# High and low weight halves in one buffer, with placements of their own for stationary and moving use

## The chip, the cores and the metric

The kernel runs on one core of a Trainium2 chip. The metric is device time in microseconds (us), the median of several executions of the whole program, from the first instruction to the last.

## The reference

Two decoder layers over 256 tokens of width 2048, batch 1, all in float32. Layer 0 mixes tokens with sparse attention (compressed blocks, selected blocks and a sliding window, gated), layer 1 with a chunkwise mLSTM. After each mixer comes a gated convolution FFN of width 5632, and a normalisation ends it.

```python
for i in range(DEPTH):                       # DEPTH = 2
    xn = rms_norm(x, norm_mix[i])
    y = nsa_mixer(...) if i % 2 == 0 else mlstm_mixer(...)
    x = x + y
    x = x + conv_glu_ffn(rms_norm(x, norm_ffn[i]), ffn_w_up[i], ...)
return rms_norm(x, norm_final)
```

In `nsa_mixer` the attention scores, of queries with compressed and with plain keys, are multiplied by `hd ** -0.5`, here `QSCALE`. Nearly all of the arithmetic is products of the 256 x K activations with large weight matrices.

## The kernel before

**Products in three parts.** TensorE's fast float32 type (`fp32r`) is not exact enough alone, so every big operand is kept as a high half (the value rounded to `fp32r`) and a low half (the rest). A product is the sum of three matmuls: high x high, low x high and high x low. The activations stand transposed in `xh` and `xl` (16 k-tiles of 128 partitions x 256 tokens). Mixer outputs stand in `oh`, `ol` (called `moh`, `mol` in the mLSTM), the FFN's hidden values in `gh`, `gl`, laid out in the same way.

**Weights on the way in.** `load_split` loads a piece of 128 partitions x up to 1024 columns from HBM into `raw` (4 buffers, DMA issued by SyncE). ScalarE writes the high half into `whi` (line 192) and VectorE the low half into `wlo` (line 194), with 5 buffers each. The pieces are split ahead of TensorE in program order; a buffer is handed on when its last reader is done.

**Three users of a piece.**

- `cols_piece` (lines 228, 230, 231) has the weights stationary and the activations moving, 256 columns: per k-tile and 128 output columns it multiplies `whi` with `xh`, `whi` with `xl` and `wlo` with `xh`. Query and key projections and the FFN's up projection take it, 24 matmuls to a piece.
- `rows_times` has the weights moving and `xh`, `xl` stationary, by `rows_mm` (lines 200 to 202): `xh` with `whi`, `xh` with `wlo`, `xl` with `whi`. It makes the value and gate projections, with 256, 304, 412, 416 or 512 columns a matmul.
- `project_out` uses `rows_mm` too, with `oh`, `gh` or `moh` (and their low halves) stationary: output projections and the FFN's down projection, 512 columns a matmul (256 in the last one for the second half of the tokens), 12 matmuls to a piece.

While a matmul streams its moving operand, the stationary operand of the next one is loaded.

**Where things lie.** A pool's tiles stand one behind the other in each partition, and buffers of a tile in a row; small unused `pad_` tiles shift what follows. `xh` and `xl` take 16384 bytes each, a multiple of 256. Counted from them, in bytes modulo 256:

| tile | before | after |
|---|---|---|
| `xh`, `xl` | 0 | 0 |
| `raw` | 64 | 0 |
| high half, weights stationary | 64 | 64 |
| low half, weights stationary | 192 | 192 |
| high half, weights moving | 64 | 0 |
| low half, weights moving | 192 | 0 |
| `oh`, `gh`, `moh` | 64 | 0 |
| `ol`, `gl`, `mol` | 192 | 0 |
| step from one weight buffer to the next, bytes | 4096 | 8448 = 33 x 256 |

In the attention's gather (lines 601 to 603) the probabilities `ph`, `pl` move, 512 columns, over the stationary values `vh`, `vl`; all four stand at one phase, before and after.

**Order of work.** Each engine runs its own instructions in program order. Side work (attention units, mLSTM heads, evacuations of accumulators) is put between pieces by a queue (`tick`). The lines that the steps below speak of: `load_split` 181 to 196, `rows_mm` 198 to 202, `rows_times` 205, `cols_piece` 221 to 232, `project_out` 312, `k_out` 424, `rq` 445, `compressed` 495, `q_out` 507.

Of the kernel before, what the change touches and what calls it, by code (L numbers as in the profile page):

```python
# [21 lines left out]
P = 128  # L22
# [40 lines left out]
def trunk(ctx: ExitStack, tc: tile.TileContext, x, positions, nsa_w_in, nsa_gate_b, nsa_cmp_pe,  # L63
# [10 lines left out]
    wpool = ctx.enter_context(tc.tile_pool(name="wpool", bufs=1))  # L74
    wpool.tile([P, 16], F32, name="pad_w")
    small = ctx.enter_context(tc.tile_pool(name="small", bufs=2))
# [4 lines left out]
    def nm(s):  # L81
        uid[0] += 1
        return f"{s}_{uid[0]}"
# [91 lines left out]
    def preload(w, k0, nk, c0, n):  # L175
        ready[w.tensor.name, w.offset, k0, c0] = load_split(w, k0, nk, c0, n)

    apart = []

    def load_split(w, k0, nk, c0, n):  # L180
        got = ready.pop((w.tensor.name, w.offset, k0, c0), None)
        if got is not None:
            return got
        view = lambda t: t[:, :nk * n].rearrange("p (k c) -> p k c", k=nk)
        raw = wpool.tile([P, 1024], F32, name=nm("raw"), tag="raw", bufs=RAWB)
        nc.sync.dma_start(view(raw), w[k0 * P:(k0 + nk) * P, c0:c0 + n].rearrange("(k p) c -> p k c", p=P))
        hi = wpool.tile([P, 1024], F32R, name=nm("whi"), tag="whi", bufs=SPB)
        if not apart:
            apart.append(wpool.tile([P, 32], F32, name="pad_lo"))
        lo = wpool.tile([P, 1024], F32R, name=nm("wlo"), tag="wlo", bufs=SPB)  # L190
        with queued("act"):
            latest["act"] = act(view(hi), view(raw), AF.Copy).ins  # L192
        with queued("ve"):
            latest["ve"] = ve.tensor_sub(view(lo), view(raw), fview(view(hi))).ins  # L194
        return view(hi), view(lo)
# [24 lines left out]
    def cols_piece(ps, w, c0, k0, n):  # L220
        hi, lo = load_split(w, k0, n, c0, 256)
        run_hooks()
        for i in range(n):
            for j in range(2):
                kt = k0 + i
                a = hi[:, i, j * P:(j + 1) * P]
                b = lo[:, i, j * P:(j + 1) * P]
                mm(ps[:, j, :], a, xh[:, kt, :], start=(kt == 0 and j == 0), stop=False,  # L228
                   skip_group_check=True)
                mm(ps[:, j, :], a, xl[:, kt, :], start=False, stop=False, skip_group_check=True)  # L230
                mm(ps[:, j, :], b, xh[:, kt, :], start=False, stop=(kt == KT - 1 and j == 1),  # L231
                   skip_group_check=True)
        tick()
# [115 lines left out]
    def nsa(norm, nxt):  # L349
        with tc.tile_pool(name="nsa", bufs=1) as pool, tc.tile_pool(name="nsw", bufs=2) as wk:  # L350
# [13 lines left out]
            gate = pool.tile([P, NT, 48], F32, name="gate")  # L364
            rq = pool.tile([P, S], F32, name="rq")
            hid = pool.tile([P, 2, 32], F32, name="hid")
# [4 lines left out]
            nc.gpsimd.memset(fview(pct), 0.0)  # L371
            pool.tile([P, 32], F32, name="pad_oh")
            oh = pool.tile([P, HEADS, S], F32R, name="oh")
            pool.tile([P, 32], F32, name="pad_ol")
            ol = pool.tile([P, HEADS, S], F32R, name="ol")
# [48 lines left out]
            def k_out(b, ps):  # L424
                ve.tensor_mul(kr[:, :, b, :], ps, norm.rbc2)
                rope(kr[:32, :, b, :], kr[:32, :, b, :])
# [11 lines left out]
            def vw_out(accs):  # L438
# [5 lines left out]
                act(gate, gate, AF.Sigmoid)  # L444
                ve.tensor_scalar(rq, norm.rbc, QSCALE, None, op0=ALU.mult)

# [48 lines left out]
            def compressed():  # L495
                ps = bank()
                mm(ps[:, :32], w2[:, 0, :], hid[:, 0, :], start=True, stop=True)
                ve.tensor_copy(kcmp.rearrange("p g j -> p (g j)"), ps[:, :32])
                ps = bank()
# [7 lines left out]
            def q_out(pair, ps):  # L507
                qu = wk.tile([P, 2, S], F32, name=nm("qu"), tag="qu", bufs=3)
                qr = wk.tile([P, 2, S], F32, name=nm("qr"), tag="qr", bufs=3)
                ve.tensor_mul(qu, ps, rq[:, None, :].to_broadcast([P, 2, S]))  # L510
                act(qr, qu, AF.Copy)
                rope(qr[:32], qu[:32])
                q[pair] = (qu, qr)
# [167 lines left out]
    def mlstm(norm, nxt):  # L681
        with tc.tile_pool(name="mls", bufs=1) as pool, tc.tile_pool(name="mlw", bufs=2) as wk:
# [6 lines left out]
            nc.gpsimd.memset(v1[:, :, :, DV:DV + 1], 1.0)  # L689
            pool.tile([P, 48], F32, name="pad_m")  # L690
            oh = pool.tile([P, KT, S], F32R, name="moh")
            pool.tile([P, 32], F32, name="pad_n")
            ol = pool.tile([P, KT, S], F32R, name="mol")
# [166 lines left out]
    def ffn(layer, norm, nxt):  # L860
        with tc.tile_pool(name=f"ffn{layer}", bufs=1) as pool, tc.tile_pool(name=f"ffw{layer}", bufs=2) as wk:
            pool.tile([P, 16], F32, name=f"pad_f{layer}")
            pads = []
            wu, wd = ffn_w_up[layer], ffn_w_down[layer]
# [18 lines left out]
            def up(ffs):  # L883
                gh = wk.tile([P, 8, S], F32R, name=nm("gh"), tag="gh")
                if not pads:
                    pads.append(wk.tile([P, 32], F32, name=f"pad_g{layer}", tag="pad_g", bufs=1))
                gl = wk.tile([P, 8, S], F32R, name=nm("gl"), tag="gl")
# [118 lines left out]
```

## Time and profile before

| what | us |
|---|---|
| median of 3 runs | 2188.14 (2188.11 to 2188.83) |
| the profiled execution | 2189.75 |
| its span, first to last instruction | 2188.0 |
| TensorE matmuls busy | 2170.5 (99%) |
| VectorE busy | 1441.2 (66%) |
| ScalarE busy | 1114.1 (51%) |
| mean granted TensorE clock, as a share of full speed | 0.996 |

A matmul's shown duration includes the way through the array and overlaps the next one, so durations of matmuls don't add up to time; the distance between starts does. What the profile calls idle before an instruction is time in which its engine ran nothing, with the event that ended it. A timeline row gives the start, the shown length, the engine, the line and the tiles.

### The profile page before, as it was taken

What the parts mean: (1) busy time and instruction counts of PE and PEld (TensorE: products, weight loads), DVE (VectorE), ACT (ScalarE), POOL (GpSimd) and SP (SyncE); (2) the same over time, 40 slices, a digit from 0 to 9 for tenths busy, and PEclk for the clock granted to TensorE, in tenths of its full rate; (3) what the DMA queues carried; (4) which work ended last, traced back from release to release, by engine and by line L of the source; (5) the groups of instructions that cost most, each with busy time, mean ns of one, the idle gap of its engine ahead of it and who ended that gap; (6) DMA issues with size and microseconds to landing.
All of it is one profiled execution on the core that took longest, in us unless ns stands there. A gap on an engine that the chain in (4) does not pass through costs nothing.

```text
span 2188.0 us, 37284 instructions
## 1 busy us (share of the span) xinstructions
PE 2170.5 (99%) x15072; PEld 1999.7 (91%) x15072; DVE 1441.2 (66%) x2191; ACT 1114.1 (51%) x1565; POOL 19.2 (1%) x56
## 2 busy tenths in 40 slices
PE   9999999999999999999999999999999999999998
PEld 8898789999989899998899988889999898998986
DVE  7488757776657666675645666667676576675755
ACT  6366655554545454453654444555545454454543
POOL 2000000000000000000000000000000000000000
PEclk9999999999999999999999999999999999999999
DMA  7653345666666666666566555566666666666664
GB/s 243 203 174 107 106 162 181 197 193 193 193 192 193 191 195 192 193 194 189 161 189 202 173 173 172 171 200 194 194 193 193 191 195 190 193 193 191 192 192 133
DMA packets 298317, 403.33 MB, mean 184 GB/s; under 512 B 12904, under 2 KB 256840, under 8 KB 298016
## 3 DMA queue, kind: packets, MB, share of 16 engines
q1 hardware_dynamic: 297264, 399.03, 58.8%
q8 instruction: 118, 1.93, 0.4%
q0 software_dynamic: 688, 1.83, 0.3%
q14 instruction: 55, 0.45, 0.1%
q10 hardware_dynamic: 192, 0.08, 0.0%
HBM read 398.80 MB, written 2.10 MB: 183 GB/s over the span
## 4 chain that ended last, share of the span: by engine, by line
PE 97%; ACT 1%; DVE 1%; DMA 1%; issue 0%; SPq 0%; ACTq 0%
PE bank L228 18%; PE bank L231 18%; PE bank L230 18%; PE bank L201 13%; PE bank L200 13%; PE bank L202 13%; PE bank L553 1%; PE bank L262 1%; ACT pr L557 0%; ACT whi L192 0%; PE bank L584 0%; DVE wlo L194 0%; DMA h<-in_x_dram 0%; PE bank L528 0%; DMA raw<-in_nsa_w_in_dram 0%; PE bank L602 0%
## 5 line engine op out<-in xcount | busy, mean ns | idle before, releaser
L194 DVE TENSOR_TENSOR wlo<-raw,whi 128x1024 fp32r<-128x1024 f32 (+3 forms) x755 | 911.8, 1209 | 591.7 <-ACT whi L192 590.6
L192 ACT ACTIVATE whi<-raw 128x1024 fp32r<-128x1024 f32 (+3 forms) x755 | 791.2, 1049 | 913.7 <-PE bank L230 429.1
L228 PE MATMUL bank<-xh,whi 128*128 128x256 f32 x3456 | 959.3, 278 | 3.1 <-ACT whi L192 1.9
L231 PE MATMUL bank<-xh,wlo 128*128 128x256 f32 x3456 | 956.1, 277 | 1.5 <-DVE wlo L194 1.5
L230 PE MATMUL bank<-xl,whi 128*128 128x256 f32 x3456 | 956.3, 277 | 0.2 <-DVE xl L268 0.2
L228 PEld LDWEIGHTS bank<-xh,whi 128*128 128x128 f32 x3456 | 650.4, 188 | 7.6 <-ACT whi L192 2.8
L231 PEld LDWEIGHTS bank<-xh,wlo 128*128 128x128 f32 x3456 | 650.4, 188 | 1.9 <-DVE wlo L194 1.9
L230 PEld LDWEIGHTS bank<-xl,whi 128*128 128x128 f32 x3456 | 650.5, 188 | 1.4 <-DVE xl L268 0.5
L201 PE MATMUL bank<-wlo,gh 128*128 128x512 f32 (+1 forms) x712 | 279.8, 393 | 0.0
L200 PE MATMUL bank<-whi,gh 128*128 128x512 f32 (+1 forms) x712 | 278.1, 391 | 0.0
L202 PE MATMUL bank<-whi,gl 128*128 128x512 f32 (+1 forms) x712 | 277.1, 389 | 0.0
L200 PEld LDWEIGHTS bank<-whi,gh 128*128 128x128 f32 x712 | 133.9, 188 | 30.9
L202 PEld LDWEIGHTS bank<-whi,gl 128*128 128x128 f32 x712 | 133.7, 188 | 30.0
L201 PEld LDWEIGHTS bank<-wlo,gh 128*128 128x128 f32 x712 | 133.6, 188 | 28.3
L200 PE MATMUL bank<-whi,xh 128*128 128x412 f32 (+4 forms) x352 | 128.2, 364 | 0.0
L202 PE MATMUL bank<-whi,xl 128*128 128x412 f32 (+4 forms) x352 | 124.8, 354 | 0.0
L201 PE MATMUL bank<-wlo,xh 128*128 128x412 f32 (+4 forms) x352 | 124.6, 354 | 0.0
L873 ACT ACTIVATE ac<-u,tapc 128x256 f32<-128x256 f32 x176 | 95.0, 587 | 3.8 <-DVE u L869 3.8
L313 DVE TENSOR_TENSOR h<-bank,h 128x512 f32<-128x512 f32 (+1 forms) x113 | 72.9, 680 | 36.3 <-PE bank L202 36.3
L869 DVE TENSOR_TENSOR u<-bank,rbc 128x512 f32<-128x512 f32 x88 | 60.8, 691 | 43.1 <-PE bank L231 43.1
L875 DVE SCALAR_TENSOR_TENSOR ac<-u,tapc,ac 128x255 f32<-128x255 f32 x176 | 77.3, 479 | 3.0 <-ACT ac L873 3.0
L877 DVE SCALAR_TENSOR_TENSOR ac<-u,tapc,ac 128x254 f32<-128x254 f32 x176 | 77.2, 478 | 0.3
(251 smaller groups left out, 1505.9 us busy)
## 6 DMA issues: line engine op xcount, KB each, us to landing
raw<-in_ffn_w_up_dram SPq DMA_DIRECT2D x352, 512.0 KB, 3.8
raw<-in_ffn_w_down_dram SPq DMA_DIRECT2D x176, 512.0 KB, 4.5
raw<-in_mlstm_w_in_dram SPq DMA_DIRECT2D x64, 512.0 KB, 3.7
raw<-in_nsa_w_in_dram SPq DMA_DIRECT2D x51, 512.0 KB, 4.5
raw<-in_nsa_w_out_dram SPq DMA_DIRECT2D x32, 512.0 KB, 3.7
raw<-in_mlstm_w_out_dram SPq DMA_DIRECT2D x32, 512.0 KB, 3.7
raw<-in_mlstm_w_in_dram SPq DMA_DIRECT2D x32, 412.0 KB, 4.0
raw<-in_nsa_cmp_w_dram SPq DMA_DIRECT2D x16, 256.0 KB, 3.3
```

The costliest lines, as they stand in the source:

```text
L192: latest["act"] = act(view(hi), view(raw), AF.Copy).ins
L194: latest["ve"] = ve.tensor_sub(view(lo), view(raw), fview(view(hi))).ins
L200: mm(o, a, hi[:, i, c:e], start=first, stop=False)
L201: mm(o, a, lo[:, i, c:e], start=False, stop=False)
L202: mm(o, b, hi[:, i, c:e], start=False, stop=last)
L228: mm(ps[:, j, :], a, xh[:, kt, :], start=(kt == 0 and j == 0), stop=False, skip_group_check=True)
L230: mm(ps[:, j, :], a, xl[:, kt, :], start=False, stop=False, skip_group_check=True)
L231: mm(ps[:, j, :], b, xh[:, kt, :], start=False, stop=(kt == KT - 1 and j == 1), skip_group_check=True)
L313: ve.tensor_add(h[:, t, a:b], acc[:, :b - a], h[:, t, a:b])
L873: act(ac[:, j, :], uu[:, j, :], AF.Identity, bias=taps[:, 3, f:f + 1], scale=taps[:, 2, f:f + 1])
L875: ve.scalar_tensor_tensor(ac[:, j, 1:], uu[:, j, :S - 1], taps[:, 1, f:f + 1], ac[:, j, 1:], op0=ALU.mult, op1=ALU.add)
L877: ve.scalar_tensor_tensor(ac[:, j, 2:], uu[:, j, :S - 2], taps[:, 0, f:f + 1], ac[:, j, 2:], op0=ALU.mult, op1=ALU.add)
```

## The change

One tile `split` of 2 x 1024 + 64 columns holds both halves, with 5 buffers. A new argument `cols` tells whether the weights will be stationary; `places` gives the two offsets in columns of 4 bytes: 16 and 48 (64 and 192 bytes) if so, 0 and 0 if not. `cols_piece` passes it, and `preload` passes it for pieces of 256 columns. The unused tiles are dropped or resized, so that `oh`, `ol`, `gh`, `gl`, `moh` and `mol` stand at the phase of `xh`. The scaled reciprocal `rq` of the attention goes: `QSCALE` is applied to the keys instead, in `k_out` and in `compressed`, and `q_out` multiplies with the plain `rbc2`. No matmul and no DMA is added, removed or moved.

```diff
-    wpool.tile([P, 16], F32, name="pad_w")
...
     def preload(w, k0, nk, c0, n):
-        ready[w.tensor.name, w.offset, k0, c0] = load_split(w, k0, nk, c0, n)
-
-    apart = []
-
-    def load_split(w, k0, nk, c0, n):
+        ready[w.tensor.name, w.offset, k0, c0] = load_split(w, k0, nk, c0, n, n == 256)
+
+    def places(w, cols):
+        if cols:
+            return 16, 48
+        return 0, 0
+
+    def load_split(w, k0, nk, c0, n, cols=False):
...
-        hi = wpool.tile([P, 1024], F32R, name=nm("whi"), tag="whi", bufs=SPB)
-        if not apart:
-            apart.append(wpool.tile([P, 32], F32, name="pad_lo"))
-        lo = wpool.tile([P, 1024], F32R, name=nm("wlo"), tag="wlo", bufs=SPB)
+        split = wpool.tile([P, 2 * 1024 + 64], F32R, name=nm("wsp"), tag="wsp", bufs=SPB)
+        a, b = places(w, cols)
+        a, b = (a, 1024 + b) if a <= b else (1024 + a, b)
+        hi, lo = split[:, a:a + 1024], split[:, b:b + 1024]
...
-        hi, lo = load_split(w, k0, n, c0, 256)
+        hi, lo = load_split(w, k0, n, c0, 256, True)
...
-            rq = pool.tile([P, S], F32, name="rq")
...
-            pool.tile([P, 32], F32, name="pad_oh")
             oh = pool.tile([P, HEADS, S], F32R, name="oh")
-            pool.tile([P, 32], F32, name="pad_ol")
             ol = pool.tile([P, HEADS, S], F32R, name="ol")
...
-                ve.tensor_mul(kr[:, :, b, :], ps, norm.rbc2)
+                ve.scalar_tensor_tensor(kr[:, :, b, :], ps, QSCALE, norm.rbc2, op0=ALU.mult, op1=ALU.mult)
...
-                ve.tensor_scalar(rq, norm.rbc, QSCALE, None, op0=ALU.mult)
...
-                ve.tensor_copy(kcmp.rearrange("p g j -> p (g j)"), ps[:, :32])
+                ve.tensor_scalar(kcmp.rearrange("p g j -> p (g j)"), ps[:, :32], QSCALE, None, op0=ALU.mult)
...
-                ve.tensor_mul(qu, ps, rq[:, None, :].to_broadcast([P, 2, S]))
+                ve.tensor_mul(qu, ps, norm.rbc2)
...
-            pool.tile([P, 48], F32, name="pad_m")
+            pool.tile([P, 16], F32, name="pad_m")
             oh = pool.tile([P, KT, S], F32R, name="moh")
-            pool.tile([P, 32], F32, name="pad_n")
...
-            pool.tile([P, 16], F32, name=f"pad_f{layer}")
-            pads = []
+            pool.tile([P, 48], F32, name=f"pad_f{layer}")
...
-                if not pads:
-                    pads.append(wk.tile([P, 32], F32, name=f"pad_g{layer}", tag="pad_g", bufs=1))
```

## Rows read from the trace of the kernel before

**Rows 1.** Page: busy us by engine, share, instructions; chain that ended last, by engine.

```profile
PE 2170.5 (99%) x15072; PEld 1999.7 (91%) x15072; DVE 1441.2 (66%) x2191; ACT 1114.1 (51%) x1565; POOL 19.2 (1%) x56
...
PE 97%; ACT 1%; DVE 1%; DMA 1%; issue 0%; SPq 0%; ACTq 0%
```

**Rows 2.** Page, costliest groups: count, busy us, mean ns, idle before and releaser.

```profile
L194 DVE TENSOR_TENSOR wlo<-raw,whi 128x1024 fp32r<-128x1024 f32 (+3 forms) x755 | 911.8, 1209 | 591.7 <-ACT whi L192 590.6
...
L192 ACT ACTIVATE whi<-raw 128x1024 fp32r<-128x1024 f32 (+3 forms) x755 | 791.2, 1049 | 913.7 <-PE bank L230 429.1
...
L231 PE MATMUL bank<-xh,wlo 128*128 128x256 f32 x3456 | 956.1, 277 | 1.5 <-DVE wlo L194 1.5
...
L200 PE MATMUL bank<-whi,gh 128*128 128x512 f32 (+1 forms) x712 | 278.1, 391 | 0.0
...
L200 PE MATMUL bank<-whi,xh 128*128 128x412 f32 (+4 forms) x352 | 128.2, 364 | 0.0
```

**Rows 3.** Groups by line and form: line 200 in the other two `project_out`.

```profile
L200 PE MATMUL bank<-whi,oh 128*128 128x512 f32 x128 | 51.3, 401 | 0.0
...
L200 PE MATMUL bank<-whi,moh 128*128 128x512 f32 x128 | 51.5, 402 | 0.0
```

**Rows 4.** TensorE by stretch: length, busy us, count, clock, DMA share, GB/s.

```profile
502.00:586.00 84.00, 84.00 (x744) 1.00 0.62 194
...
590.00:630.00 40.00, 40.00 (x175) 1.00 0.61 187
...
1095.00:1163.00 68.00, 68.00 (x366) 1.00 0.69 197
```

**Rows 5.** Timeline, FFN `project_out`, line 200: start us, shown length us.

```profile
999.94 0.39 PE L200 MATMUL bank<-whi,gh 128*128 128x512 f32 x1
...
1000.62 0.40 PE L200 MATMUL bank<-whi,gh 128*128 128x512 f32 x1
...
1001.32 0.39 PE L200 MATMUL bank<-whi,gh 128*128 128x512 f32 x1
```

**Rows 6.** Timeline, attention gather, two chains: first and last, 6 and 5 matmuls.

```profile
173.41 0.39 PE L602 MATMUL bank<-pl,vh 128*128 128x512 f32 x1
...
174.57 0.28 PE L228 MATMUL bank<-xh,whi 128*128 128x256 f32 x1
...
250.25 0.40 PE L602 MATMUL bank<-pl,vh 128*128 128x512 f32 x1
...
251.16 0.40 PE L603 MATMUL bank<-ph,vl 128*128 128x512 f32 x1
```

**Rows 7.** Timeline, `rows_times` of 256 columns: first and last of ten matmuls.

```profile
41.82 0.28 PE L202 MATMUL bank<-whi,xl 128*128 128x256 f32 x1
...
42.88 0.28 PE L202 MATMUL bank<-whi,xl 128*128 128x256 f32 x1
```

**Rows 8.** Timeline, last `project_out` piece, 256 columns: first and last of ten.

```profile
2176.02 0.28 PE L202 MATMUL bank<-whi,gl 128*128 128x256 f32 x1
...
2177.08 0.28 PE L202 MATMUL bank<-whi,gl 128*128 128x256 f32 x1
```

**Rows 9.** Timeline, `rows_times` of 512 columns: first and last of 27.

```profile
1165.90 0.39 PE L200 MATMUL bank<-whi,xh 128*128 128x512 f32 x1
...
1171.89 0.39 PE L202 MATMUL bank<-whi,xl 128*128 128x512 f32 x1
```

**Rows 10.** Waits: total us, times, longest us.

```profile
ACT whi L192 <- PE bank L230: 429.1, 324, 2.1
```

**Rows 11.** Two source lines: count, duration ns min/median/max, first and last start.

```profile
L445 DVE TENSOR_SCALAR rq<-rbc x1: 284/284/284, 49.4 to 49.4; 128x256 f32<-128x256 f32 x1
...
L425 DVE TENSOR_TENSOR kr<-bank,rbc x2: 691/692/692, 78.6 to 99.7; 128x512 f32<-128x512 f32 x2
```

**Rows 12.** Timeline, mLSTM `project_out`: first and last of nine matmuls.

```profile
1425.06 0.40 PE L200 MATMUL bank<-whi,moh 128*128 128x512 f32 x1
...
1426.91 0.40 PE L202 MATMUL bank<-whi,mol 128*128 128x512 f32 x1
```

## The prediction

> **What bounds the kernel now.** I read the page's busy times and its chain first. TensorE is busy for 99% of the span and its own work is 97% of the chain that ended last [rows 1]. VectorE, at 66%, and ScalarE, at 51%, run beside it. So the time is the number of matmuls times the distance between their starts (the pitch below), and a change counts only if it moves a pitch or starves TensorE.
>
> The groups by line, read next, give the counts [rows 2, 3]. With the weights stationary (lines 228, 230, 231) there are 3 x 3456 = 10368 matmuls of 256 columns. With the weights moving (lines 200 to 202) there are 3 x (712 + 128 + 128) = 2904 in `project_out` and 3 x 352 = 1056 in `rows_times`. Their durations there are no pitch, since consecutive matmuls overlap.
>
> The pitch comes from stretches that hold one kind alone, at the full granted clock [rows 4]. A window counts each matmul that touches it, so its length plus one shown matmul, over the count, is the pitch. The stationary stage gives (84.00 + 0.28) / 744 = 113.3 ns, `project_out` (40.00 + 0.40) / 175 = 230.8 ns and the 412-column stage (68.00 + 0.35) / 366 = 186.8 ns. At 2.4 GHz, 256, 512 and 412 columns would take 106.7, 213.3 and 171.7 ns, so 6 to 9% of each matmul is something else; the change could get at that.
>
> **What the change moves.** Call the byte offset within a partition, modulo 256 and counted from `xh` and `xl`, the phase. From the tile sizes, the phases before and after are:
>
> - Stationary weights: high 64, low 192 against moving activations at 0. The same after.
> - `project_out`: before, moving high 64 and low 192 against stationary high 64 and low 192; after, all at 0. The difference stays 0.
> - `rows_times`: before, moving high 64 and low 192 against stationary 0, so stationary minus moving is 192, 64, 192 in the three products. After, 0, 0, 0. With 304, 412 and 416 columns the later k-slices of a piece are displaced further, before and after.
>
> **Stationary stages.** 10368 x 113.3 ns = 1175 us. Every difference modulo 256 is kept: 0 us. This rests on the period being 256 bytes (a rival below).
>
> **`project_out`.** 2904 x 230.8 ns = 670 us. The difference is kept, but now the streams follow each other at one phase, where before they stepped by 128 bytes between high and low. This could matter, because the triples alternate: starts of line 200 lie 0.68 and then 0.70 us apart [rows 5], and so on in turn. The nearest rows with everything at one phase are in the attention's gather (lines 601 to 603, 512 columns; `vh`, `vl`, `ph`, `pl` all share a phase). One chain there runs (174.57 - 173.41) / 5 = 232.0 ns, another (251.16 - 250.25) / 4 = 227.5 ns [rows 6]. They lie on both sides of 230.8, and short chains after a wait are poorer samples than 175 matmuls of the same instructions; I take 230.8, so 0 us, with bounds 2904 x (-3.3, +1.2) = -9.6 to +3.5 us.
>
> **`rows_times`.** These 1056 matmuls do get another difference.
>
> - 256 columns, 96 matmuls: difference 192, 64, 192 gives (42.88 - 41.82) / 9 = 117.8 ns [rows 7]. In the last `project_out`, 256 columns wide, difference 0 gives (2177.08 - 2176.02) / 9 = 117.8 ns [rows 8]. Nothing gained: 0 us.
> - 512 columns, 384 matmuls: now (1171.89 - 1165.90) / 26 = 230.4 ns [rows 9], against 230.8 ns at difference 0: 384 x 0.4 = +0.2 us.
> - 412 columns, 384 matmuls: the straight line through 117.8 at 256 and 230.8 at 512 columns is 186.7 ns, against 186.8 now: 0 us. Half of these pieces, the second slice, land at a difference of 144, which no row shows.
> - 304 and 416 columns, 96 each: taken at 0 us, being too few to matter.
>
> For the unseen part I let the whole group, 384 x (230.8 + 186.7) + 96 x (117.8 + 139.0 + 188.4) ns = 203 us (the last two from the same line), vary by the spread of the gather, -1.4 to +0.5%: -2.8 to +1.0 us.
>
> **A rule of the skill.** The rows show that the columns alone do not set the pitch: with 256 columns it is 113.3 ns when activations move [rows 4] and 117.8 ns when weights move [rows 7]. The Trainium skill, in "TensorE: Matmul & The Clock Gate", Part 2 (Step-by-step), says that TensorE has two independent SBUF read ports and that loading the next weights takes no read bandwidth from the running matmul. By that rule no placement could matter, and the sum would be the 2188.1 of before. It gives no reason for the two pitches, so the trace speaks for something that the rule leaves out; it speaks against this change all the same.
>
> **The shared buffer.** High and low are now handed back together. In the stationary stages line 231 reads last, one matmul after line 230, so ScalarE's next high split starts 0.113 us later; it spends 429.1 us over 324 waits on line 230 now [rows 10]. Behind it on its queue stand the later splits and evacuations; VectorE's low split waits for it in any case. It is hidden: five buffers leave four pieces of 24 x 0.113 = 2.7 us, 10.9 us of matmuls, ahead of a split of about 1.1 us on ScalarE and 1.2 us on VectorE (estimates from 791.2 and 911.8 us over 755 splits) [rows 2]. TensorE waited 1.5 us in total for low halves [rows 2]. Cost 0; were the cover gone, 432 pieces x 0.113 = +49 us. If reads of the high half had to wait for the low half too, only the pieces where TensorE starves now would pay two matmuls, 0.23 us each: under 2 us.
>
> **The scaling.** `rq`, 0.28 us, goes; `k_out`'s two multiplications of 0.69 us get a second factor; `kcmp` is scaled as it is copied [rows 11]. All on VectorE, which idles a third of the span: 0 us. If the cover were gone, a few tenths of a us either way.
>
> **The sum.** The profiled execution took 2189.75 us, 1.75 above its span and 1.6 above the median of 2188.14. Its change is 0 + 0 + 0.2 + 0 = +0.2 us, which taken to the median makes 2188.3 us. A measurement of this kernel can tell about 0.2%, 4.4 us, from no change.
>
> **Rivals.**
>
> - *The alternation locks to its short half* (faster). With all streams at one phase every triple could be a 0.68 and none a 0.70. Half of 968 + 128 triples of 512 columns, 548, would save 0.02 us or a little more (by the two-digit starts): 548 x 0.0225 = -12 us, 2176 us. For it: short triples exist. Against: the gather chain of 232.0 at one phase.
> - *The pattern repeats in 512 bytes, not in 256* (slower). Before, weight buffers step by 4096 bytes; after, by 8448 = 33 x 256, so every second buffer lies 256 bytes off modulo 512. If that makes a pair clash in the stationary stages, two or three of five buffers pay 117.8 instead of 113.3 ns: 10368 x 0.5 x 4.5 ns = +23 us, 2212 us. It decides as soon as some buffers show over 114 ns. Against: in the mLSTM's `project_out` the stationary tile already lies 256 off modulo 512, and runs (1426.91 - 1425.06) / 8 = 231 ns [rows 12], no worse than the 230.8 of the FFN's.
> - *It locks to the long half* (slower): the same 548 triples the other way, +12 us, 2200 us.
> - *The joint hand-back shows* (slower): +49 us, 2237 us, if the look-ahead is shorter than the rows say.
> - *The change does nothing to the streams at all*: 2188.1 us, in the same case as my forecast.
>
> **Chances.** No change within 4.4 us: 0.70. Faster: 0.19, of which 0.14 for the short lock and 0.05 for a part of it, within the gather's bounds. Slower: 0.11, of which 0.05 for the 512-byte period, 0.04 for the long lock and 0.02 for the hand-back. The likeliest is 2188.3 us. The bounds of the terms, -12.4 and +4.5 us, reach from 2176 to 2193, and the short lock lies at the lower end; so the range is 2175 to 2194 us, which leaves out the slow rivals alone.
>
> **What would show it.** The same windows of the changed kernel should count again about 744 matmuls in 84 us of a stationary stage, 175 in 40 us of `project_out` and 366 in 68 us of the 412 columns. More than 177 in `project_out` means the short lock, fewer than 740 in the stationary stage the 512-byte period, idle time of TensorE behind `wlo` the hand-back. I am wrong if a pitch moves by more than 1% in the first two stages, or if TensorE's idle time grows beyond some 2 us.

## The result and the profile after

The changed kernel takes 2175.84 us (median of 6 runs, 2175.3 to 2178.18) against 2188.72 us (6 runs, 2188.11 to 2190.16): a ratio of 0.9942, 95% interval 0.9932 to 0.9952. That is 12.9 us faster, three times what was called measurable. The forecast was no change, 2188.3 us; the time is the one given for the rival "the alternation locks to its short half", 2176 us, and lies at the lower end of the range of 2175 to 2194 us.

The profiled execution took 2176.23 us, its span 2174.4 us, 13.6 us less than before. The first fence has the page's busy times, its chain by engine and its groups, to be laid beside [rows 1] and [rows 2]. Line numbers are two higher for the split (194 and 196), `rows_mm` (202 to 204) and the stationary stages (230, 232, 233), and both halves are called `wsp`.

```profile
PE 2158.6 (99%) x15072; PEld 1998.6 (92%) x15072; DVE 1439.6 (66%) x2190; ACT 1114.6 (51%) x1565; POOL 19.0 (1%) x56
...
PE 98%; DMA 1%; DVE 0%; SPq 0%; ACT 0%; issue 0%; ACTq 0%
...
L196 DVE TENSOR_TENSOR wsp<-raw,wsp 128x1024 fp32r<-128x1024 f32 (+3 forms) x755 | 912.0, 1209 | 591.7 <-ACT wsp L194 590.8
L194 ACT ACTIVATE wsp<-raw 128x1024 fp32r<-128x1024 f32 (+3 forms) x755 | 791.9, 1050 | 917.6 <-PE bank L233 436.1
...
L233 PE MATMUL bank<-xh,wsp 128*128 128x256 f32 x3456 | 955.5, 277 | 1.5 <-DVE wsp L196 1.5
...
L202 PE MATMUL bank<-wsp,gh 128*128 128x512 f32 (+1 forms) x712 | 276.0, 388 | 0.0
...
L202 PE MATMUL bank<-wsp,xh 128*128 128x412 f32 (+4 forms) x352 | 127.4, 362 | 0.0
```

The same work, in the same counts, still fills TensorE for 99% of a shorter span. The splits take what they took, and TensorE waits the same 1.5 us for low halves. So it is the matmuls that stand closer. Which ones is told by the first and the last start of line 200 (now 202) in the three uses of `project_out`. First before, then after; the columns are shortest/median/longest shown length in ns, first and last start in us, and the shapes, whose counts aren't used here.

```profile
L200 PE MATMUL bank<-whi,oh x128: 387/396/478, 232.5 to 345.5; 128*128 128x512 f32 x128
...
L200 PE MATMUL bank<-whi,gh x712: 274/395/477, 478.1 to 2178.6; 128*128 128x512 f32 x174, 128*128 128x256 f32 x4
...
L200 PE MATMUL bank<-whi,moh x128: 387/397/583, 1357.5 to 1453.7; 128*128 128x512 f32 x128
```

```profile
L202 PE MATMUL bank<-wsp,oh x128: 387/389/482, 231.1 to 342.7; 128*128 128x512 f32 x128
...
L202 PE MATMUL bank<-wsp,gh x712: 277/389/481, 475.4 to 2165.1; 128*128 128x512 f32 x174, 128*128 128x256 f32 x4
...
L202 PE MATMUL bank<-wsp,moh x128: 389/389/591, 1349.8 to 1444.7; 128*128 128x512 f32 x128
```

Start minus start gives the lead of the changed kernel: 1.4 us when the attention's `project_out` begins, 2.8 when it ends, 2.7 when the first FFN's begins, 7.7 at the mLSTM's, 9.0 at its end, 13.5 at the last one of the second FFN. The lead grows by 1.4 and 1.3 us in the two short `project_out` stages, by 5.0 and 4.5 us over the stretches that hold an FFN, and not between 345.5 and 478.1 us, where no `project_out` runs. The 1.4 us before all of them is told at the end.

Now the distances themselves. The timeline of TensorE (start in us, shown length in us, engine, line, operation, tiles) gives the first long stretch of `project_out` in the first FFN. From the first to the last of these rows it is 180 matmuls in each kernel. Before:

```profile
589.52 0.40 PE L200 MATMUL bank<-whi,gh 128*128 128x512 f32 x1
...
631.12 0.40 PE L200 MATMUL bank<-whi,gh 128*128 128x512 f32 x1
```

After, with three consecutive starts of line 202 out of its middle, to be laid beside [rows 5]:

```profile
586.32 0.39 PE L202 MATMUL bank<-wsp,gh 128*128 128x512 f32 x1
...
604.00 0.39 PE L202 MATMUL bank<-wsp,gh 128*128 128x512 f32 x1
...
604.68 0.39 PE L202 MATMUL bank<-wsp,gh 128*128 128x512 f32 x1
...
605.36 0.39 PE L202 MATMUL bank<-wsp,gh 128*128 128x512 f32 x1
...
627.12 0.39 PE L202 MATMUL bank<-wsp,gh 128*128 128x512 f32 x1
```

180 matmuls took 41.60 us, 231.1 ns each, and take 40.80 us now, 226.7 ns each. Where triples of 0.68 and 0.70 us took turns, all now take 0.68. The other stages are seen in windows, with length, TensorE's busy time and count, its weight loads, the busy times of VectorE, ScalarE and GpSimd, the granted clock, the DMA share and GB/s:

```profile
510.00:580.00 70.00, 70.00 (x620) 70.00 (x619) 49.77 (x66) 38.25 (x46) 0.00 (x0) 1.00 0.64 194
...
1095.00:1155.00 60.00, 60.00 (x320) 59.33 (x320) 27.36 (x27) 28.66 (x34) 0.00 (x0) 1.00 0.72 194
```

The stationary stage gives (70.00 + 0.28) / 620 = 113.4 ns, as before, and the 412-column stage (60.00 + 0.35) / 320 = 188.6 ns, up from 186.8 [rows 4].

### The profile page after: what moved, and what is told of

It reads as the page before. It is cut to its first block, busy times and chain, and to the rows that moved or that the text cites. A ratio compares the mean times of both kernels' runs of the same rounds, so it can differ in the third digit from the quotient of the medians.

```text
span 2174.4 us, 37271 instructions
## 1 busy us (share of the span) xinstructions
PE 2158.6 (99%) x15072; PEld 1998.6 (92%) x15072; DVE 1439.6 (66%) x2190; ACT 1114.6 (51%) x1565; POOL 19.0 (1%) x56
## 4 chain that ended last, share of the span: by engine, by line
PE 98%; DMA 1%; DVE 0%; SPq 0%; ACT 0%; issue 0%; ACTq 0%
PE bank L230 18%; PE bank L232 18%; PE bank L233 18%; PE bank L204 13%; PE bank L202 13%; PE bank L203 13%; PE bank L551 1%; DMA raw<-in_nsa_w_in_dram 1%; PE bank L264 1%; PE bank L582 0%; DMA h<-in_x_dram 0%; PE bank L526 0%; PE bank L600 0%; PE bank L599 0%; PE bank L601 0%; DVE wsp L196 0%
## 5 line engine op out<-in xcount | busy, mean ns | idle before, releaser
L196 DVE TENSOR_TENSOR wsp<-raw,wsp 128x1024 fp32r<-128x1024 f32 (+3 forms) x755 | 912.0, 1209 | 591.7 <-ACT wsp L194 590.8
L194 ACT ACTIVATE wsp<-raw 128x1024 fp32r<-128x1024 f32 (+3 forms) x755 | 791.9, 1050 | 917.6 <-PE bank L233 436.1
L230 PE MATMUL bank<-xh,wsp 128*128 128x256 f32 x3456 | 958.5, 277 | 1.4 <-ACT xh L269 0.6
L233 PE MATMUL bank<-xh,wsp 128*128 128x256 f32 x3456 | 955.5, 277 | 1.5 <-DVE wsp L196 1.5
L232 PE MATMUL bank<-xl,wsp 128*128 128x256 f32 x3456 | 955.5, 277 | 0.1
L230 PEld LDWEIGHTS bank<-xh,wsp 128*128 128x128 f32 x3456 | 649.8, 188 | 5.9 <-issue 1.9
L233 PEld LDWEIGHTS bank<-xh,wsp 128*128 128x128 f32 x3456 | 649.7, 188 | 1.9 <-DVE wsp L196 1.9
L232 PEld LDWEIGHTS bank<-xl,wsp 128*128 128x128 f32 x3456 | 649.9, 188 | 1.2 <-DVE xl L270 0.4
L202 PE MATMUL bank<-wsp,gh 128*128 128x512 f32 (+1 forms) x712 | 276.0, 388 | 0.0
L203 PE MATMUL bank<-wsp,gh 128*128 128x512 f32 (+1 forms) x712 | 275.5, 387 | 0.0
L204 PE MATMUL bank<-wsp,gl 128*128 128x512 f32 (+1 forms) x712 | 275.4, 387 | 0.0
L202 PEld LDWEIGHTS bank<-wsp,gh 128*128 128x128 f32 x712 | 133.7, 188 | 26.9
L203 PEld LDWEIGHTS bank<-wsp,gh 128*128 128x128 f32 x712 | 133.7, 188 | 26.6
L202 PE MATMUL bank<-wsp,xh 128*128 128x412 f32 (+4 forms) x352 | 127.4, 362 | 0.0
L203 PE MATMUL bank<-wsp,xh 128*128 128x412 f32 (+4 forms) x352 | 124.7, 354 | 0.0
```

The costliest lines, as they stand in the source:

```text
L202: mm(o, a, hi[:, i, c:e], start=first, stop=False)
L203: mm(o, a, lo[:, i, c:e], start=False, stop=False)
L204: mm(o, b, hi[:, i, c:e], start=False, stop=last)
```

## The experiments

Each experiment is the changed kernel with one edit, except where the kernel before is named. Ratios are to the kernel before on the same chip, with their 95% interval. Where `project_out` is moved, the two timeline rows bound the same stretch of 180 `project_out` matmuls as above; their difference is the figure to compare with 41.60 and 40.80 us.

### Is it the shared buffer or the places in it?

The changed kernel with the old phases: moving halves at 64 and 192, `oh`, `gh`, `moh` at 64 and their low halves at 192.

```diff
-        return 0, 0
+        return 16, 48
...
+            pool.tile([P, 16], F32, name="pad_oh")
+            pool.tile([P, 32], F32, name="pad_ol")
...
-            pool.tile([P, 16], F32, name="pad_m")
+            pool.tile([P, 32], F32, name="pad_m")
+            pool.tile([P, 32], F32, name="pad_n")
...
-            pool.tile([P, 48], F32, name=f"pad_f{layer}")
+            pool.tile([P, 64], F32, name=f"pad_f{layer}")
+            pads = []
...
+                if not pads:
+                    pads.append(wk.tile([P, 32], F32, name=f"pad_g{layer}", tag="pad_g", bufs=1))
```

> The changed kernel, shared buffer, scaling and all, with the phases of the kernel before put back: moving weights at 64 (high) and 192 (low), and the stationary oh, gh, moh at 64, ol, gl, mol at 192. Theory A, that the step of 128 bytes between the streams of high and low makes the 12 us: project_out goes back to about 231 ns a matmul (175 in 40 us) and the time to 2186 to 2189 us. Theory B, that the shared buffer (its step of 8448 bytes, its common hand-back) makes them: 227 ns and 2175 to 2177 us.

Measured: 2187.81 us (10 runs), ratio 0.9994 (0.9985 to 1.0003).

```profile
589.77 0.40 PE L202 MATMUL bank<-wsp,gh 128*128 128x512 f32 x1
...
631.37 0.40 PE L202 MATMUL bank<-wsp,gh 128*128 128x512 f32 x1
```

41.60 us again. The buffer that both halves share, the larger step between buffers and the moved scaling are all in this kernel and change nothing measurable. The gain is the placement alone.

### Does the absolute phase count?

All of `project_out` at 64 instead of 0, so that the moving operand of `rows_times` no longer has the phase of `xh`.

```diff
-        return 0, 0
+        return 16, 16
...
+            pool.tile([P, 16], F32, name="pad_oh")
...
-            pool.tile([P, 16], F32, name="pad_m")
+            pool.tile([P, 32], F32, name="pad_m")
...
-            pool.tile([P, 48], F32, name=f"pad_f{layer}")
+            pool.tile([P, 64], F32, name=f"pad_f{layer}")
```

> The changed kernel with moving weights, high and low, at 64 instead of 0, and all of oh, ol, gh, gl, moh, mol at 64 too. No step between streams, but another phase against xh and xl and another place modulo 256. Theory A (only the step counts): project_out stays at 227 ns, time 2174 to 2179 us. Theory C (these tiles must lie at the phase of xh): back to about 231 ns and 2186 to 2189 us. rows_times of 512 columns now has a difference of 192 in all three products; by theory A it too stays near 228 ns.

Measured: 2175.76 us (4 runs), ratio 0.9941 (0.9924 to 0.9958).

```profile
585.32 0.39 PE L202 MATMUL bank<-wsp,gh 128*128 128x512 f32 x1
...
626.12 0.39 PE L202 MATMUL bank<-wsp,gh 128*128 128x512 f32 x1
```

40.80 us, and the time of the changed kernel. Neither the phase itself nor that of `xh` in `rows_times` carries the gain that can be measured; how the operands of `project_out` stand to one another does.

### Step on one side

First the moving low half is put 128 bytes behind the high one, the stationary side staying at 0.

```diff
-        return 0, 0
+        return 0, 32
```

> The changed kernel with the low half of the moving weights 128 bytes further, all stationary tiles left at 0. A step on the moving side alone, and a difference of 128 in the product that follows. Theory A with the moving side deciding: project_out at 230 ns or more, time 2184 us or more. If only a step on the stationary side counts: 227 ns and about 2176 us.

Then the stationary low halves instead (`ol`, `gl`, `mol`), the moving side staying at 0.

```diff
+            pool.tile([P, 32], F32, name="pad_ol")
...
+            pool.tile([P, 32], F32, name="pad_n")
...
+            pads = []
...
+                if not pads:
+                    pads.append(wk.tile([P, 32], F32, name=f"pad_g{layer}", tag="pad_g", bufs=1))
```

> The changed kernel with ol, gl and mol 128 bytes further, the moving weights left at 0. A step on the stationary side alone, in project_out only; rows_times is as in the changed kernel. If the stationary side decides: project_out at 230 ns or more, time 2184 us or more. If only the moving side counts: 227 ns and about 2176 us.

Measured: 2188.61 us (10 runs), ratio 0.9997 (0.9988 to 1.0006), and 2187.75 us (10 runs), ratio 0.9992 (0.9983 to 1.0001). The rows of the moving step, then of the stationary one:

```profile
586.89 0.39 PE L202 MATMUL bank<-wsp,gh 128*128 128x512 f32 x1
...
628.49 0.39 PE L202 MATMUL bank<-wsp,gh 128*128 128x512 f32 x1
```

```profile
587.74 0.39 PE L202 MATMUL bank<-wsp,gh 128*128 128x512 f32 x1
...
629.34 0.39 PE L202 MATMUL bank<-wsp,gh 128*128 128x512 f32 x1
```

41.60 us in both. A step of 128 bytes on either side costs the whole gain, and the step on both sides (the kernel before) costs just as much. A step always brings a difference with it, because each low half is multiplied with a high one: in the three products, stationary minus moving is 0, 128, 0 with the moving step, 0, 0, 128 with the stationary one, and 0, 128, 128 in the kernel before (modulo 256).

The trace of the stationary step shows where the time goes. In its stretch the starts of line 203 lie 226.7 ns behind those of line 202 on average (60 pairs), which is the pitch of the changed kernel. Those of line 204, which has the displaced `gl`, lie 232.7 ns behind line 203, and those of the next line 202 lie 234.0 ns behind line 204.

### A steady difference without a step

In the next three kernels the moving halves stay at 0 and all stationary tiles of `project_out` move together, to 128, 64 and 192. This is the edit for 128; for 64 the three pads have 16, 32 and 64 columns, for 192 they have 48, 64 and 96.

```diff
+            pool.tile([P, 32], F32, name="pad_oh")
...
-            pool.tile([P, 16], F32, name="pad_m")
+            pool.tile([P, 48], F32, name="pad_m")
...
-            pool.tile([P, 48], F32, name=f"pad_f{layer}")
+            pool.tile([P, 80], F32, name=f"pad_f{layer}")
```

> The changed kernel with all stationary tiles of project_out, high and low, 128 bytes away from the moving weights, which stay at 0. No step between streams on either side, but a difference of 128 where the change has 0. Theory A (steps count, the difference does not): 227 ns, 2174 to 2179 us. Theory E (both count: no step and difference 0): 230 ns or more, 2184 us or more.

> As e9_as_in_cols without the step: oh, ol, gh, gl, moh, mol all at 64, moving weights at 0, difference 64 in all three products. Theory 'equal phases are best': the difference costs, as 128 bytes did in e8_apart_128; 180 matmuls take 41.2 to 41.9 us and the time is 2182 to 2191 us. Rival 'as in the stationary stages' (a difference of 64 leaves the smaller gap): 39.6 us for 180 matmuls, about 2157 us.

> As e10_apart_64 with oh, ol, gh, gl, moh, mol at 192, moving weights at 0, difference 192 in all three products. Theory 'equal phases are best': the 512-column pieces of rows_times in e2_all_64, also at a steady difference of 192, ran at 229.2 ns; at that pitch 180 matmuls take 41.3 us and the time is about 2176 + 2904 x 2.3 ns = 2182 to 2183 us. Rival 'as in the stationary stages': 39.6 us for 180 matmuls, about 2157 us.

A fourth takes over the phases of the stationary stages, moving at 0, stationary at 64 (high) and 192 (low): the pads of the kernel with the old places, with `return 0, 0` kept.

> The changed kernel with the phases of the stationary stages in project_out: moving weights at 0 as before this edit, stationary oh, gh, moh at 64 and ol, gl, mol at 192, so that stationary minus moving is 64, 64, 192 in the three products, the sequence that the stationary stages run at 113.3 ns. Theory 'equal phases are best': any step of 128 bytes in the stationary operand brings the long triples back, as in e4_step_stationary; 180 matmuls of the first long stretch of project_out take some 41.6 us instead of 40.8, and the time is 2186 to 2190 us. Rival 'as in the stationary stages': what counts is the sequence of differences, and 64, 64, 192 leaves a smaller gap after each matmul than equal phases do (113.3 ns there against 119.9 ns at equal phases, 6.6 ns); then 180 matmuls take 39.6 us and the time falls by up to 2904 x 6.6 ns = 19 us, to about 2157 us.

Measured: 2190.9 us at 128 (10 runs), ratio 1.0005 (0.9996 to 1.0014); 2192.85 us at 64 (10 runs), 1.0014 (1.0005 to 1.0024); 2181.86 us at 192 (5 runs), 0.9965 (0.9952 to 0.9978); 2189.18 us at 64 and 192 (10 runs), 0.9999 (0.9989 to 1.0008). The rows in that order:

```profile
589.18 0.40 PE L202 MATMUL bank<-wsp,gh 128*128 128x512 f32 x1
...
631.01 0.39 PE L202 MATMUL bank<-wsp,gh 128*128 128x512 f32 x1
```

```profile
588.12 0.40 PE L202 MATMUL bank<-wsp,gh 128*128 128x512 f32 x1
...
630.12 0.40 PE L202 MATMUL bank<-wsp,gh 128*128 128x512 f32 x1
```

```profile
586.96 0.39 PE L202 MATMUL bank<-wsp,gh 128*128 128x512 f32 x1
...
628.16 0.39 PE L202 MATMUL bank<-wsp,gh 128*128 128x512 f32 x1
```

```profile
587.80 0.39 PE L202 MATMUL bank<-wsp,gh 128*128 128x512 f32 x1
...
629.53 0.39 PE L202 MATMUL bank<-wsp,gh 128*128 128x512 f32 x1
```

These are 41.83, 42.00, 41.20 and 41.73 us. Equal phases without a step remain the best that was tried, 192 without a step the second best. The expectation for 192 (41.3 us, 2182 to 2183 us) nearly held; 64 came out a little beyond its range (41.9 us, 2191 us), slower than the kernel before, and 128 no faster than it. The rival, that the placement of the stationary stages would also be the best here, falls: what serves 256 moving columns doesn't serve 512.

### Would one placement for both uses do?

First the kernel before, with separate buffers and every pad dropped that set low halves apart, so that all weights and all of `project_out` lie at 64. The stationary stages then have 64 and 64 where they had 64 and 192.

```diff
-        if not apart:
-            apart.append(wpool.tile([P, 32], F32, name="pad_lo"))
...
-            pool.tile([P, 32], F32, name="pad_oh")
-            pool.tile([P, 32], F32, name="pad_ol")
...
-            pool.tile([P, 48], F32, name="pad_m")
+            pool.tile([P, 16], F32, name="pad_m")
...
-            pool.tile([P, 32], F32, name="pad_n")
...
-            pool.tile([P, 16], F32, name=f"pad_f{layer}")
-            pads = []
+            pool.tile([P, 48], F32, name=f"pad_f{layer}")
...
-                if not pads:
-                    pads.append(wk.tile([P, 32], F32, name=f"pad_g{layer}", tag="pad_g", bufs=1))
```

> The kernel before with its separate buffers and its own scaling, but with the padding between high and low buffers taken out, so that both halves of the weights lie at 64, and the mixer and FFN tiles, high and low, at 64 too. Moving weights have no step now; stationary weights lie at 64 and 64 instead of 64 and 192. Theory A (no step in the moving products makes all of it, and the stationary stages don't care about the 192): project_out at 227 ns, stationary stages at 113.4 ns, 2174 to 2179 us without any shared buffer. Theory D (the stationary stages need 64 and 192): project_out at 227 ns, but the stationary stages lose; at 117.8 ns they would cost 10368 x 4.4 ns = 46 us, 2222 us.

Then the changed kernel with stationary weights at 0 and 0, so that everything has one phase.

```diff
-            return 16, 48
+            return 0, 0
```

> The changed kernel with stationary weights, high and low, at 0 too, the phase of xh and xl, as if the placement were one for all uses. Theory A' (the stationary stages don't care where their weights lie): 113.4 ns and 2174 to 2179 us. Theory D (they need 64 and 192): slower, up to 117.8 to 120 ns a matmul, which is 46 to 68 us, 2222 to 2244 us.

Measured: 2207.01 us (4 runs), ratio 1.0079 (1.0064 to 1.0094), and 2240.74 us (4 runs), ratio 1.0232 (1.0215 to 1.0249). The stretch of `project_out` in the first (its line 196 is `rows_mm`):

```profile
594.84 0.39 PE L196 MATMUL bank<-whi,gh 128*128 128x512 f32 x1
...
635.64 0.39 PE L196 MATMUL bank<-whi,gh 128*128 128x512 f32 x1
```

The window of a stationary stage in it:

```profile
510.00:580.00 70.00, 70.00 (x597) 70.00 (x596) 47.20 (x62) 36.22 (x43) 0.00 (x0) 1.00 0.61 185
```

The same window in the second:

```profile
510.00:580.00 70.00, 70.00 (x586) 70.00 (x585) 45.15 (x57) 34.61 (x42) 0.00 (x0) 1.00 0.60 185
```

`project_out` gains without any shared buffer, 40.80 us. But the stationary stage falls from 620 matmuls in 70 us to 597 (117.7 ns) and 586 (119.9 ns). Over the whole kernel that is (2207.01 - 2175.84) / 10368 = 3.0 ns a matmul in the first and (2240.74 - 2175.84) / 10368 = 6.3 ns in the second.

The 3.0 ns are less than the window's 117.7 - 113.4 = 4.3 ns, because the first kernel doesn't have the long pitch everywhere. An earlier window of it, in the stretch ahead of its first `project_out` in the FFN:

```profile
410.00:470.00 60.00, 60.00 (x532) 60.00 (x531) 41.86 (x54) 31.62 (x38) 0.00 (x0) 1.00 0.63 192
```

That is (60.00 + 0.28) / 532 = 113.3 ns, the pitch of 64 and 192, with the weights at 64 and 64. Its trace has two unbroken runs of 1008 stationary matmuls that settle at 113.3 ns and eight of 768 that hold 117.8 ns from first to last, which is why the expected 2222 us was not reached. Both pitches are open to the same placement, and what decides between them isn't settled. At 64 and 192 all ten of these runs settle at 113.3 ns.

So the placements that serve moving use best serve stationary use worse. Of the three tried for stationary weights only 64 and 192 has the short pitch in every long run, and a buffer whose halves are placed by use lets both uses have what they need.

### The slices inside a piece

With 304, 412 and 416 columns the second and later slices of a piece lie at other phases. Here each slice starts at a multiple of 256 bytes.

```diff
+        step = -(-n // 64) * 64
+        part = lambda t: t[:, :nk * step].rearrange("p (k c) -> p k c", k=nk)[:, :, :n]
...
-            latest["act"] = act(view(hi), view(raw), AF.Copy).ins
+            latest["act"] = act(part(hi), view(raw), AF.Copy).ins
...
-            latest["ve"] = ve.tensor_sub(view(lo), view(raw), fview(view(hi))).ins
-        return view(hi), view(lo)
+            latest["ve"] = ve.tensor_sub(part(lo), view(raw), fview(part(hi))).ins
+        return part(hi), part(lo)
```

> The changed kernel with the k-slices of moving weights that are 304, 412 or 416 columns wide put at a step of 320 or 448 columns in the split buffer, so that each slice begins at phase 0 (before and after the change the second slice of 412 columns begins 112 bytes further). If a step between slices is what keeps the 412-column stage from its floor: about 183 ns instead of 188, 384 x 5 ns = 2 us less, 2173 to 2174 us. If the width of 412 itself does: no change, 2175 to 2177 us.

Measured: 2175.95 us (4 runs), ratio 0.9936 (0.9921 to 0.9951), no different from the changed kernel. The 412-column window:

```profile
1095.00:1155.00 60.00, 60.00 (x323) 60.00 (x322) 27.67 (x27) 28.78 (x34) 0.00 (x0) 1.00 0.71 198
```

(60.00 + 0.35) / 323 = 186.8 ns against 188.6: the displaced slices are what made the 412 columns slower, but 384 x 1.8 ns = 0.7 us is too little to show in the time. The pitch lies between the two expectations, 5 ns less and no change.

### The placements of `project_out` side by side

The column "difference" gives stationary minus moving, modulo 256 bytes, in the three products.

| kernel | moving high, low | stationary high, low | difference | 180 matmuls, us | ns each |
|---|---|---|---|---|---|
| before, and old places | 64, 192 | 64, 192 | 0, 128, 128 | 41.60 | 231.1 |
| changed | 0, 0 | 0, 0 | 0, 0, 0 | 40.80 | 226.7 |
| all at 64, two kernels | 64, 64 | 64, 64 | 0, 0, 0 | 40.80 | 226.7 |
| step in the moving | 0, 128 | 0, 0 | 0, 128, 0 | 41.60 | 231.1 |
| step in the stationary | 0, 0 | 0, 128 | 0, 0, 128 | 41.60 | 231.1 |
| apart by 64 | 0, 0 | 64, 64 | 64, 64, 64 | 42.00 | 233.3 |
| apart by 128 | 0, 0 | 128, 128 | 128, 128, 128 | 41.83 | 232.4 |
| apart by 192 | 0, 0 | 192, 192 | 192, 192, 192 | 41.20 | 228.9 |
| as in the stationary stages | 0, 0 | 64, 192 | 64, 64, 192 | 41.73 | 231.8 |

The short pitch appears where no product has a difference between its sides, and only there. A difference costs without any step, as the three kernels apart by 64, 128 and 192 show. Whether a step costs something of its own isn't shown, since none can be had here without a difference. What in the reading of operands makes it so isn't settled; differences other than multiples of 64, and a step with other differences, weren't tried.

## Why the prediction was wrong

- **What bounds the kernel** was right: TensorE's pitch. All that was gained was gained there, and VectorE and ScalarE kept their times.
- **Stationary stages, 0 us:** right, 113.4 ns against 113.3. The rival with a period of 512 bytes falls: buffers of 33 x 256 bytes stand here, and the mean of 620 matmuls is the old pitch.
- **`project_out`, 0 us with bounds -9.6 to +3.5:** this is the step that failed, and in two places. "The difference stays 0" isn't so. Counted product by product, as the prediction counts `rows_times`, stationary minus moving was 0, 128, 128 before, since each low half meets a high one, and is 0, 0, 0 after: the change takes away what the experiments show to cost 4.4 ns a matmul. With the difference taken as kept, one point remained, that the streams now follow one another at one phase, and it was sized by the gather's two short chains [rows 6], of which the slow one, 232.0 ns, stood against the short lock. Such chains don't show the steady pitch, and with starts to 0.01 us a chain of four or five leaves its pitch open by some 2 ns. The changed kernel's own `rows_times` shows why: here is a run of 512 columns just after smaller matmuls, its second, seventh and last row.

```profile
1169.28 0.39 PE L203 MATMUL bank<-wsp,xh 128*128 128x512 f32 x1
...
1170.44 0.39 PE L202 MATMUL bank<-wsp,xh 128*128 128x512 f32 x1
...
1174.30 0.39 PE L204 MATMUL bank<-wsp,xl 128*128 128x512 f32 x1
```

  The first five take (1170.44 - 1169.28) / 5 = 232.0 ns each, the gather's number to the digit; the next seventeen (1174.30 - 1170.44) / 17 = 227.1 ns. This stream starts slow and settles, and a chain of five ends before it does. It isn't so for every run: the one that starts at 1157.74 us has (1159.78 - 1157.74) / 9 = 226.7 ns up to the row at 1159.78 us that is shown below. Whether the gather's chains were slow for that reason alone wasn't tried. In the long stretch the term is 231.1 - 226.7 = 4.4 ns, up to 2904 x 4.4 = 12.9 us; over all undisturbed neighbouring matmuls of both traces, the starts of runs among them, the mean fell by 4.2 ns for `gh` and by some 3 ns for `oh` and `moh`, in all 11.0 us. That lies outside the lower bound.
- **`rows_times`, +0.2 us with bounds -2.8 to +1.0:** inside, but by luck: the terms nearly cancel. The 512 columns fell from 230.4 ns [rows 9] to (1168.39 - 1159.78) / 38 = 226.6 ns in an undisturbed run; with the starts of runs among them the mean fell by 2.4 ns, 0.9 us in all. The 412 columns rose by 0.6 to 0.7 us, through the slices at 144, the place that "no row shows". The 256 columns, "nothing gained", rose from 117.8 ns [rows 7] to (43.48 - 40.85) / 22 = 119.5 ns, 0.2 us. The rows of the first and the last of these:

```profile
40.85 0.28 PE L203 MATMUL bank<-wsp,xh 128*128 128x256 f32 x1
...
43.48 0.28 PE L204 MATMUL bank<-wsp,xl 128*128 128x256 f32 x1
...
1159.78 0.39 PE L202 MATMUL bank<-wsp,xh 128*128 128x512 f32 x1
...
1168.39 0.39 PE L204 MATMUL bank<-wsp,xl 128*128 128x512 f32 x1
```

- **The shared buffer and the scaling, 0 us each:** right, as the kernel with the old places shows (0.9994), which has both. ScalarE's wait for the last reader is now put down to line 233, 436.1 us against 429.1 [rows 10], and nobody is held up by it.
- **The rule weighed there** ("TensorE: Matmul & The Clock Gate", Part 2, Step-by-step, in the Trainium skill: two independent read ports, so that loading the next weights takes nothing from the running matmul) would have left every placement at the same pitch. The runs contradict that consequence: from phases alone, the stationary stage went from 113.4 to 119.9 ns and `project_out` from 226.7 to 233.3 ns. The prediction had noticed that the rule explained neither of its two pitches, and still let it count against the change.
- **The rivals:** the short lock happened, at the price worked out for it, 12 us, because its premise ("every triple could be a 0.68 and none a 0.70") was taken from the rows of the stage itself [rows 5]. Its chance of 0.14 was too low, given that the only row against it came from a chain of five. The long lock, the joint hand-back and "nothing at all" fall.
- **What would show it:** TensorE's idle time answered as foreseen. The counts in the named windows didn't answer, since the changed kernel is ahead there and its windows already hold matmuls of the next stage. It counts 188 in 590 to 630 us, and 736 in 502 to 586 us, which is under the 740 that were to show the 512-byte period although the pitch of that stage hasn't changed: 510 to 580 us lies within it in both kernels and holds 620 matmuls in both. Equal work, 180 matmuls from first to last, does.

The sum by parts is -11.0 for `project_out`, -0.9, +0.7 and +0.2 for `rows_times` (304 and 416 columns, under 0.2 us together, left out): -11.0 us, against 12.9 between the medians. Between the two profiled executions 13.6 us are missing. Of these, 1.4 were there before the first `project_out`, where executions differ by that much without the change (next section); the rest of 1.2 us isn't assigned.

## What to carry to other kernels

Where TensorE is the bound and back-to-back matmuls stand several per cent above their columns, try the placement of both operands modulo 256 bytes, for each use on its own: here it was worth 2% of a `project_out` matmul, and the wrong one costs the stationary stages 6%. Take the pitch of a steady stream from equal work in long runs of that very stream, not from short chains behind a wait. Count the difference product by product, not half by half. An alternation in the rows (0.68, 0.70) shows a shorter state that the same instructions can reach, so price it and look for what would hold it.

## What the runs showed of the hardware

At the full granted clock of 2.4 GHz the steady pitches at equal phases, and that of the stationary stages at 64 and 192, come out as whole cycles above the columns. Equal phases leave 32 cycles a matmul for both widths: 226.7 ns is 544 = 512 + 32, and 119.9 ns (stationary weights at 0 and 0) is 288 = 256 + 32, as the 119.5 ns of `rows_times` nearly is. The stationary stages at 64 and 192 need half of it, 113.3 ns or 272 = 256 + 16. At 64 and 64 they run at this pitch or at 117.8 ns, each for a whole run. Before, a `project_out` triple took 41.60 / 60 = 693.3 ns or 1664 cycles, 32 more than the 1632 now. So equal phases are the best found for 512 moving columns and the worst found for 256 in the stationary stage.

The surplus is gone at half the clock. The kernel before, in its profiled execution, has a stretch at a lower granted clock, and so has the kernel with everything at 64. These windows are of the one and of the other:

```profile
86.40:89.50 3.10, 3.10 (x16) 3.10 (x16) 0.92 (x1) 0.00 (x0) 0.00 (x0) 0.50 0.81 235
```

```profile
85.60:88.20 2.60, 2.60 (x14) 2.60 (x14) 0.90 (x1) 0.00 (x0) 0.00 (x0) 0.50 0.72 211
```

The granted clock is 0.50 of full speed in both, the level of 1.2 GHz; the changed kernel has 1.00 from 81 to 97 us. So the stretch comes with the new placement as well as with the old and is no work of the change. In the kernel before, TensorE had waited twice for halves of weights just ahead of it. In its timeline the first row is the second of these waits, the other two bound 15 matmuls:

```profile
85.66 0.38 PE L231 MATMUL bank<-xh,wlo 128*128 128x256 f32 x1 [0.76 <-DVE wlo L194]
...
86.36 0.41 PE L230 MATMUL bank<-xl,whi 128*128 128x256 f32 x1
...
89.57 0.36 PE L230 MATMUL bank<-xl,whi 128*128 128x256 f32 x1
```

They take (89.57 - 86.36) / 15 = 214.0 ns each, and 256 columns at 1.2 GHz are 213.3 ns: the 16 cycles that this stage pays at full clock are not there. The stretch cost 15 x (214.0 - 113.3) ns = 1.5 us. That is about the changed kernel's lead of 1.4 us before its first `project_out`, but it doesn't explain the lead. Two kernels with no difference in any product of `project_out` show this. The first row is of the one with everything at 64, which has the slow stretch, and the second of the one with the slices at 0, which has 1.00 from 81 to 97 us:

```profile
L202 PE MATMUL bank<-wsp,oh x128: 389/389/478, 230.1 to 341.8; 128*128 128x512 f32 x128
```

```profile
L204 PE MATMUL bank<-wsp,oh x128: 387/389/482, 232.5 to 344.1; 128*128 128x512 f32 x128
```

The one with the slow stretch arrives first, at 230.1 us, and the other at 232.5 us like the kernel before. So before the first `project_out` the executions differ by 2 us for reasons that aren't settled, and the lead of 1.4 us there can't be put down to the change or to the clock.
